# One step of a hybrid mLSTM/HGRN2 encoder on one core: HGRN score copies to ScalarE, a power on GpSimd for the head norms, later splits of fourth sums and embeddings

## The chip, the cores and the metric

The kernel runs on one core of one Trainium2 chip. The metric is device time in microseconds (us) of one execution, the median over several runs. Engines are named as in the profile: PE is TensorE's matmul array, PEld its weight loader, DVE is VectorE, ACT is ScalarE, POOL is GpSimd, and SP is the sync engine, which here only issues transfers (DMAs). Each engine works through a queue of its own in a fixed order; an instruction that waits holds everything behind it on that engine. All arithmetic is 32-bit; the matmuls take 32-bit operands split into a high and a low part.

## The reference, cut to what matters

One layer of a streaming encoder is computed for a prompt (512 frames of a new stream) and a sample (32 frames of a running stream). Both go through the same `_trunk`; an mLSTM branch and an HGRN2 branch run side by side and are merged. The parts that the change touches are the HGRN2 branch, the merge gates and the embeddings:

```python
xn = _rmsnorm(h, norm_g[l])
proj = xn @ w_in[l]
u, v_m, z_m, ig_pre, fg_pre, q_h, f_h, i_h, g_h, ga, gb = jnp.split(proj, _split_points(), axis=-1)
...
lfh = jnp.log(lb + (1.0 - lb) * jax.nn.sigmoid(f_lin))
kh = (1.0 - lb) * jax.nn.sigmoid(-f_lin)
qh = jax.nn.silu(q_h.astype(f32))
oh, S_new = _hgrn(to_heads(qh), to_heads(kh), to_heads(i_h.astype(f32)), to_heads(lfh), S0[l].astype(f32))
oh = _head_rmsnorm(oh.transpose(0, 2, 1, 3), hnorm_g[l].astype(f32)) * jax.nn.silu(g_h.astype(f32))
yb = oh.astype(x.dtype) @ w_brh[l]
y = jax.nn.sigmoid(ga) * ya + jax.nn.sigmoid(gb) * yb
h = h + y @ w_out[l]
h = h + jax.nn.sigmoid(h @ w_pg[l]) * (p[l] @ w_ple[l])
```

```python
def _hgrn_chunk(S, inp):
    q, k, v, lf = inp
    ...
    g = jnp.cumsum(lf, axis=2)
    dec = jnp.exp(jnp.where(causal, g[:, :, :, None, :] - g[:, :, None, :, :], -jnp.inf))
    a = jnp.einsum('bhtc,bhtsc,bhsc->bhts', q, dec, k)
    o = jnp.einsum('bhtc,bhce->bhte', q * jnp.exp(g), S) + jnp.einsum('bhts,bhse->bhte', a, v)
```

There are 8 HGRN heads of 128 channels. Each head's output is normalised by the root of its mean square over 128 channels (`_head_rmsnorm`). The embeddings `p` have 256 channels and are multiplied with `w_ple` at the end.

## The kernel before, in words

**Stages.** After the input norm the kernel works through four mLSTM heads (up to about 630 us), then through the HGRN loop with the merge gates (to about 960 us), and then through the dense products `yb` (w_brh), `o` (w_out), `ple` (w_ple) and `pg` (w_pg), the last mLSTM memories and the final norm.

**Precision.** `split` (line 101) and `split_piece` (125) divide a 32-bit operand into a high part, which is a copy on ACT (lines 103 and 130), and a low part, the difference, which is a subtraction on DVE (lines 104 and 131). Each product is three matmuls: high by high, high by low, low by high.

**Input products in pairs.** Class `Two` (387) computes two output tiles of `xn @ w_in` by a scheme with seven block products in place of eight. Besides the plain quarters a11, a12 and a22 of the weights it needs four sums of quarters, s1 to s4, which are made first and then split like the others. A block is 12 matmuls on PE. In the HGRN loop the pairs are "early" (all but the first): `begin` (397) loads one quarter by SP (line 402) and adds the other by an accumulating transfer that POOL issues (403), for s1 and s3. s2 is one more addition on DVE (`form`, 454, helper line 448). The fourth sum, s4, is s2's tile with another quarter added by an accumulating transfer that POOL issues as soon as s2 has been split (460); it uses the same buffer. The sums have five buffers (NSUM). After each block `keep` (496) copies the result from PSUM to a tile `t` on ACT (499), or `put` (502) combines it with an earlier one (506, 508, 510).

**The order of the blocks.** Class `Pump` (551) puts the blocks of all pairs into one list by due times. A pair's blocks fall due at 0 (a11), 1 (a12), 4 (s2, with s1's split), 5 (s1), 6 (s3), 9 (a22) and 10 (s4), and the next pair starts at 7. In the steady state the order is s2, s1, s3 of one pair, a11, a12 of the next, a22, s4 of the first, then s2 of the next. `prepare` (580) makes the weights, that is, emits loads, sums and splits, for the blocks up to AHEAD = 3 past the one that is about to run. `steps` (596) calls it before each block. The ACT instructions of a preparation are put behind the last `km` copy of the HGRN chain (`pump.behind`, 498), by `issue_after`.

**The HGRN chain.** `chain(h)` (1483) is the code of one head; the values that it yields say how many half blocks of the pump run on PE in between. The decay products within a chunk of 128 frames are built over seven levels c = 1, 2, 4, ..., 64. At each level ACT copies a strided key part to `km` (1500), PE multiplies it with the queries into a PSUM tile `pl` (1511), DVE multiplies decays into keys and queries (1535) and copies the scores whose pair of frames belongs to this level from PSUM into `at`, under a mask (`copy_predicated`, 1542). `at` is cleared by POOL before (1487). At the fifth level the sample's 32 frames are added (1519 to 1546). The previous head is finished inside the chain at that level too: `finish(h - 1)` (1654) transposes the normalised output on PE (`hoT`, 1659 and 1660) and multiplies by the gate. After the last level POOL cuts `at` to its two strict triangles `aa` (`triangle`, 1476, line 1479). PE transposes keys and values (`ht`, 1587), forms the state (`su`, 1606) and the output (`ho`, 1630 to 1634). Then the head norm follows: sums of squares on ACT (1641, 1642), a scaling (1643), `rsqrt` on five columns (160; integer first guess at 164 and 165, three Newton rounds at 167 to 169) and two multiplications (1645 and 1651), all on DVE.

**Merge gates and embeddings.** The last eight pairs of the pump are `ga` and `gb`. `merge_a` (1445) takes the sigmoid on ACT (1446), loads a `ya` tile and multiplies on DVE (1449); the eight products are collected in `gated`. Lines 1685 to 1690 load two embedding tiles `p` and split them into `ps0` and `ps1`, under `issue_after` on the third last product. `ple_units` (1692) uses them.

**Who orders what.** Within `tc.manual_schedule` the engines named there keep the order of the program; in the HGRN loop that is PE alone. Everything else is ordered ahead of the run by a scheduler that goes by readiness and by place in the program; `tc.high_priority()` puts instructions ahead of that place. `tc.issue_after(x)` puts instructions behind x. Semaphores and waits for buffers follow from the data.

Of the kernel before, what the change touches and what calls it, by code (L numbers as in the profile page):

```python
# [9 lines left out]
F32 = mybir.dt.float32  # L10
# [4 lines left out]
ALU = mybir.AluOpType  # L15
AX = mybir.AxisListType

P = 128
# [3 lines left out]
NP = 512  # L22
# [6 lines left out]
NB = NP // P  # L29
VW = HD + 4  # L30
VH = VW // 2
EPS = 1e-6
# [12 lines left out]
LEAD = 3  # L45
NPIECE = 5
AHEAD = 3
SCRATCH = 1024
RAWAHEAD = 4
WQ = 256  # L50
# [14 lines left out]
def hybrid_step(ctx: ExitStack, tc: tile.TileContext, a, o):  # L65
    nc = tc.nc
    V, S, G, PE = nc.vector, nc.scalar, nc.gpsimd, nc.tensor

    cp = ctx.enter_context(tc.tile_pool(name="cp", bufs=1))
# [8 lines left out]
    def slot(name, dt=F32):  # L78
        return sp.tile([P, SLOT], dt, tag="s", name=name)
# [5 lines left out]
    def small(name, shape, dt=F32, bufs=2, tag=None):  # L85
        return tp.tile(shape, dt, tag=tag or name, name=name, bufs=bufs)
# [11 lines left out]
    def paux(name):  # L98
        return pa.tile([P, 2, 512], F32, tag="a", name=name)

    def split(src, name):
        hi, lo = slot(name + "h", F32R), slot(name + "l", F32R)
        S.copy(hi[:, :T], src)
        V.tensor_tensor(lo[:, :T], src, hi[:, :T].bitcast(F32), ALU.subtract)
        return hi, lo
# [54 lines left out]
    def rsqrt(y, v, p, n, iters=3):  # L160

        t = small("rsq_t", [P, 8], I32)
        u = small("rsq_u", [P, 8])
        V.tensor_scalar(t[:p, :n], v.bitcast(I32), 1, None, ALU.logical_shift_right)
        V.tensor_scalar(y.bitcast(I32), t[:p, :n], -1, 0x5F3759DF, ALU.mult, ALU.add)
        for _ in range(iters):
            V.tensor_tensor(u[:p, :n], y, y, ALU.mult)
            V.scalar_tensor_tensor(u[:p, :n], u[:p, :n], -0.5, v, ALU.mult, ALU.mult)  # L168
            V.scalar_tensor_tensor(y, u[:p, :n], 1.5, y, ALU.add, ALU.mult)
# [29 lines left out]
    G.memset(ones, 1.0)  # L199
    zero4 = cp.tile([P, 4], F32, name="zero4")  # L200
    G.memset(zero4, 0.0)
    one4 = cp.tile([P, 4], F32, name="one4")
    G.memset(one4, 0.0)
    G.memset(one4[:, 0:1], 1.0)
# [125 lines left out]
    class One:  # L330
# [56 lines left out]
    class Two:  # L387
# [45 lines left out]
        def make(self, *forms):  # L433
            def go(raw):
                with tc.high_priority() if self.apart else nullcontext():
                    for form in forms:
                        if form not in self.w:
                            self.form(form, raw)

            return go  # L440

        def form(self, form, raw):
# [108 lines left out]
    class Pump:  # L551
# [28 lines left out]
        def prepare(self, upto):  # L580
            while self.made < min(upto, self.limit or len(self.order)):
                b = self.order[self.made]
                while self.begins and self.begins[0][0] <= self.made:
                    self.begins.pop(0)[1].begin()
                if b[1]:
                    need = self.loads.index(b[1][-1]) + 1
                    for u, i in self.loads[self.loaded : need + RAWAHEAD]:
                        self.raw[u, i] = raw_piece(w_in[u][:, i * WP : (i + 1) * WP], f"wi{u}r{i}")
                    self.loaded = max(self.loaded, min(need + RAWAHEAD, len(self.loads)))
                if b[2]:  # L590
                    after = self.pairs if isinstance(self.todo[self.ids[self.made][0]], Two) and self.pairs else self.behind
# [596 lines left out]
    with tc.manual_schedule(engines={mybir.EngineType.Activation, mybir.EngineType.DVE, mybir.EngineType.PE}):  # L1188
# [15 lines left out]
        for k in range(KD):  # L1204
            t = xt[k]
# [129 lines left out]
    with tc.manual_schedule(engines={mybir.EngineType.PE}):  # L1335
        for h in range(MH):
# [44 lines left out]
    NA = NP // 2  # L1381
# [12 lines left out]
    gbs, yas, gated = [None] * KD, [None] * KD, []  # L1394
# [88 lines left out]
    def chain(h):  # L1483

        tf, kk, q0, qq, kq, ii = (hs[h][k] for k in ("tf", "kk", "q0", "qq", "kq", "ii"))
        at = tp.tile([P, NA + P], F32, tag="bc", name=f"at{h}")
        G.memset(at, 0.0)
        snap = small("snap", [P, 2, QUADS, NS], bufs=1, tag="ksm")
        dg = small("dg", [P, 5])
        told = tf[:, :T]  # L1490
# [3 lines left out]
        for li, c in enumerate(LEVELS):  # L1494
            smp = li == QUADS
            n = HB if smp else NA
# [12 lines left out]
            pn = paux(f"pl{h}{c}")  # L1509
# [16 lines left out]
            with tc.high_priority():  # L1526
                for t, lo, m, first, _ in sides:

                    x = view(
                        kk, lo + first * c, ((qoff + (1 - 2 * first) * c, 2), (2 * c, m), (1, c))  # L1530
                    )
                    d = bass.AP(
                        t.tensor, t.offset + 1 - first, [list(t.ap[0]), [2 * first - 1, 2], [2, m], [0, c]]
                    )
                    V.tensor_tensor(x, x, d, ALU.mult)  # L1535
                if told.shape[-1] == 2 * (nb + na):
                    t = told.rearrange("p (n t) -> p n t", t=2)
# [4 lines left out]
                V.copy_predicated(at[:, :n], lmask[:, li, :n], pn[:, 0, :n])  # L1542
# [8 lines left out]
            if li == 0:  # L1551

                yield 1
                pn = paux(f"pd{h}")
# [22 lines left out]
        ov = kq  # L1577
        osb = small("osb", [P, P])
# [25 lines left out]
        for b in range(NB):  # L1604
            c = slice(b * P, (b + 1) * P)
# [22 lines left out]
        for b, (c, i, j) in enumerate(chunks):  # L1628
            d = slice(b * P, (b + 1) * P)
# [13 lines left out]
        V.tensor_scalar(hv, hv, 1.0 / P, EPS, ALU.mult, ALU.add)  # L1643
        rsqrt(hr, hv, P, 5)
        V.tensor_tensor(
            ov[:, :NP].rearrange("p (b e) -> p b e", b=NB),
            ov[:, :NP].rearrange("p (b e) -> p b e", b=NB),
            hr[:, :NB].rearrange("p (b o) -> p b o", o=1).to_broadcast([P, NB, P]),
            ALU.mult,
        )  # L1650
        V.tensor_scalar(osb, osb, hr[:, NB : NB + 1], None, ALU.mult)
        hs[h].update(ov=ov, osb=osb)

    def finish(h):
# [31 lines left out]
    for k in range(2):  # L1686
        t = slot(f"p{k}")
        with tc.issue_after(gated[-3].ins):
            nc.sync.dma_start(t[:, :T], a["pT"][k])
            ps_.append(split(t[:, :T], f"ps{k}"))  # L1690

    def ple_units(n):
# [24 lines left out]
    for f in range(KD):  # L1717
        t = slot(f"h1{f}")
# [167 lines left out]
```

## Time and profile before

| what | us |
|---|---|
| median of 3 runs | 1140.07 (1138.1 to 1141.18) |
| the profiled execution's own time | 1136.01 |
| its span, from the first to the last instruction | 1134.3 |
| PE busy in the span | 1116.8 |
| DVE busy | 896.5 |
| ACT busy | 680.2 |
| POOL busy | 185.9 |

The granted TensorE clock was 1.0 of full speed in nearly the whole span. The profile is one execution; times in it run from the start of its span. An engine that is idle shows in brackets how long it was idle before an instruction and what ended that: `[2.48 <-DMA p<-in_pT]` is 2.48 us of idle time ended by the transfer of `p`. A group's row has the line, the engine, the operation, `out<-in` by the program's names, the count, the busy time and the mean duration in ns. A row of waits has the waiting engine and line, whom it waited for, the total in us, how many times, and the longest.

### The profile page before, as it was taken

Reading aid. Unit: us, or ns where it says so; the run is one execution under the profiler, and the core shown is the slowest. Engines: PE = TensorE matmul, PEld = TensorE weight load, DVE = VectorE, ACT = ScalarE, POOL = GpSimd, SP = SyncE. Lnnn points to the kernel's source line nnn. Section 1 sums busy time; section 2 is a strip of 40 time slices with the busy share of each in tenths; the row PEclk is TensorE's granted clock in tenths of the full one; section 3 lists DMA queues with packets and bytes.
Section 4 is the critical chain, followed back from the end, with each engine's and each line's share of the span. In section 5 each row is a group of like instructions: output and inputs, shape, how many; then the busy total and the mean of one; then the engine's idle time right before and its main releaser. Section 6 shows DMA issues by size and latency. Waiting matters only on the chain.

```text
span 1134.3 us, 24068 instructions
## 1 busy us (share of the span) xinstructions
PE 1116.8 (98%) x8849; PEld 1101.4 (97%) x8849; DVE 896.5 (79%) x2027; ACT 680.2 (60%) x1537; POOL 185.9 (16%) x363
## 2 busy tenths in 40 slices
PE   9999999999999999999999999999999999999998
PEld 8999999999999999999999999999998999999998
DVE  6887998576896786976888699999999867654585
ACT  5677557655666555665665477677766657333462
POOL 4842010100010100101000122223232220000000
PEclk9999999999999999999999999999999999999999
DMA  7134224323344142552767766666666686332743
GB/s 236 56 96 133 79 75 159 118 95 106 132 152 151 49 131 105 158 168 69 239 163 234 180 145 143 138 140 140 148 149 165 174 222 172 113 103 70 269 141 116
DMA packets 91006, 159.68 MB, mean 141 GB/s; under 512 B 10245, under 2 KB 17797, under 8 KB 90889
## 3 DMA queue, kind: packets, MB, share of 16 engines
q1 hardware_dynamic: 80928, 140.27, 38.3%
q0 software_dynamic: 9792, 17.83, 10.1%
q8 instruction: 69, 1.13, 0.4%
q14 instruction: 49, 0.39, 0.1%
q10 hardware_dynamic: 168, 0.06, 0.0%
HBM read 133.21 MB, written 24.91 MB: 139 GB/s over the span
## 4 chain that ended last, share of the span: by engine, by line
PE 78%; DVE 10%; DMA 5%; ACT 3%; issue 2%; POOL 0%; SPq 0%; ACTq 0%; DVEq 0%
PE d L485 29%; PE ya L151 8%; PE pg L1736 4%; PE q L151 4%; PE yb L151 4%; PE o L151 4%; PE C L902 4%; PE k L151 4%; DMA ws<-in_w_in 3%; PE sc L862 3%; PE nm L1077 2%; PE pl L1511 2%; PE d L370 1%; DVE cv L634 1%; PE ple L151 1%
## 5 line engine op out<-in xcount | busy, mean ns | idle before, releaser
L403 POOL DMA_DIRECT2D ws<-in_w_in x46 | 40.3, 876 | 230.3 <-DVE rsq_u L168 30.3
L499 ACT COPY t<-d 128x272 f32<-128x272 f32 x126 | 47.7, 379 | 3.2 <-PE d L485 3.1
L1535 DVE TENSOR_TENSOR hkq<-hkq,q 128x288 f32<-128x288 f32 (+1 forms) x96 | 40.8, 432 | 3.9 <-PE pl L1519 1.0
L634 DVE SCALAR_TENSOR_TENSOR cv<-ub,vec,cv 128x547 f32<-128x547 f32 x48 | 40.4, 842 | 1.3 <-ACT cv L629 0.6
L1511 PE MATMUL pl<-hkq,km 128*128 128x128 f32 x224 | 38.0, 292 | 1.8 <-ACT km L1500 1.7
L1511 PEld LDWEIGHTS pl<-hkq,km 128*128 128x128 f32 x224 | 31.1, 189 | 3.9 <-ACT km L1500 3.4
L1500 ACT COPY km<-hkq 128x256 f32<-128x256 f32 x56 | 24.0, 428 | 15.6 <-DVE hkq L1535 6.2
L1006 DVE SCALAR_TENSOR_TENSOR c<-c,wi,Cs 128x258 f32<-128x258 f32 x32 | 15.3, 479 | 20.0 <-PE Cs L1004 19.8
L460 POOL DMA_DIRECT2D ws<-in_w_in x22 | 23.2, 1055 | 41.0 <-DVE ws272l L131 27.4
L914 ACT COPY Co<-C 128x258 f32<-128x258 f32 x32 | 10.4, 378 | 29.1 <-PE C L902 22.3
L1145 DVE TENSOR_TENSOR y<-ya,y 128x272 f32<-128x272 f32 x48 | 19.1, 436 | 10.3 <-PE ya L151 9.2
L1542 DVE COPY_PREDICATED at<-lmask,pl 128x256 f32<-128x256 uint8 (+1 forms) x56 | 25.3, 451 | 0.0
L1088 ACT COPY y<-nm 128x516 f32<-128x516 f32 x16 | 9.5, 591 | 21.6 <-PE nm L1077 21.5
L799 POOL COPY vsm<-vt 128x96 f32<-128x96 f32 x16 | 6.0, 382 | 88.2 <-ACT vt L510 44.7
L1479 POOL TENSOR_SCALAR_AFFINE_SELECT aa<-at 128x128 f32<-128x128 f32 x32 | 18.8, 621 | 8.9 <-DVE at L1542 8.9
L1077 PE MATMUL nm<-vhl,sh 128*128 128x258 f32 x112 | 18.3, 285 | 0.0
L1036 DVE BATCH_NORM_STATS2 bs<-y 128x6 f32<-128x512 f32 (+1 forms) x20 | 13.8, 688 | 5.5 <-ACT y L1088 5.5
L1723 DVE TENSOR_TENSOR h<-o,h 128x272 f32<-128x272 f32 x16 | 6.3, 436 | 14.5 <-PE o L151 14.5
L978 POOL CAST vhl<-one 128x4 fp32r<-128x4 f32 x8 | 2.0, 244 | 95.8 <-PE nm L1077 95.8
L876 ACT CAST sh<-dm 128x512 fp32r<-128x512 f32 (+3 forms) x16 | 7.3, 459 | 16.6 <-DVE dm L870 16.6
L1641 ACT ACTIVATE osq<-kq 128x128 f32<-128x128 f32 x32 | 9.8, 305 | 12.3 <-DVE kq L1636 12.1
L1710 DVE TENSOR_TENSOR gb<-yb,gb 128x272 f32<-128x272 f32 x16 | 6.3, 436 | 13.1 <-PE yb L151 13.1
(4490 smaller groups left out, 5072.9 us busy)
## 6 DMA issues: line engine op xcount, KB each, us to landing
ws<-in_w_in POOLq DMA_DIRECT2D x68, 256.0 KB, 4.8
ws<-in_w_in SPq DMA_DIRECT2D x46, 256.0 KB, 3.6
ya_d<-y SPq DMA_DIRECT2D x32, 272.0 KB, 2.7
y<-ya_d SPq DMA_DIRECT2D x24, 272.0 KB, 3.7
c<-in_C SPq DMA_DIRECT2D x16, 258.0 KB, 3.9
out_Cp<-Co SPq DMA_DIRECT2D x16, 258.0 KB, 2.5
out_Cs<-c SPq DMA_DIRECT2D x16, 258.0 KB, 2.8
x<-in_xT SPq DMA_DIRECT2D x8, 272.5 KB, 4.7
```

Of the source, the lines that this page charges most:

```text
L151: PE.matmul(both[b][:m, :TH], part(w, off + k * step, m, x), xx[:, half(b)], start=(k == 0 and j == 0), stop=(k == n - 1 and j == 2),)
L403: G.dma_start(t, w_in[u][:, i * WP : (i + 1) * WP], accum_op=ALU.add)
L485: PE.matmul(ps, ww[:, c], xx, start=(start and k == 0 and j == 0), stop=end, skip_group_check=not start,)
L499: S.copy(t, ps)
L634: V.scalar_tensor_tensor(cv[:, :547], ub[:, j : j + 547], vcol(V_CW + 4 * ft + j), cv[:, :547], ALU.mult, ALU.add)
L862: PE.matmul(pn[:, 0, :n], ks[f][x][:, j * P : (j + 1) * P], qs[f][y][:, NS + j * P : T], start=(f == 0 and i == 0), stop=(f == KH - 1 and ...
L902: PE.matmul(pn[g][:, :VH], kw[b][x][:, f * P : (f + 1) * P], vv[b][y][:, g * VH : (g + 1) * VH], start=(b == 0 and j == 0), stop=(b == NB ...
L1077: PE.matmul(pn[:, g, :VH], st[j][x][:, (i - j) * P : (i - j + 1) * P], vv[j][y][:, g * VH : (g + 1) * VH], start=(j == 0 and q == 0), stop ...
L1511: PE.matmul(pn[:, 0, b * P : (b + 1) * P], km[:, b * P : (b + 1) * P], view(qq, b * P, ((2 * c, P // (2 * c)), (HB + c, 2), (1, c))), star ...
L1535: V.tensor_tensor(x, x, d, ALU.mult)
L1542: V.copy_predicated(at[:, :n], lmask[:, li, :n], pn[:, 0, :n])
L1736: PE.matmul(ps, part(w, k * P, P, x), xx[:, c], start=(k == 0 and j == 0), stop=(k == KD - 1 and j == 2))
```

## The change

Four edits are made in one step.

1. *Scores.* At the first level and at the last one the masked copy on DVE is replaced by copies on ACT: one of 128x256 at the first level, and two of 64 partitions by 2x64 columns at the last. At the first level more is copied than before; the later triangles and levels take it away or write over it. Since the first level now writes the first 256 columns of `at`, POOL clears only the other 128.
2. *Norm.* The scaling moves from DVE to POOL, and the first guess with its three Newton rounds becomes a power of -0.5 on POOL with one Newton round on DVE (`newton` has the default `iters=1`; the 5 is the number of columns). The whole, with the multiplications, gets high priority. A constant of 128x5 is set at the start.
3. *Fourth sums.* The preparation of an early pair's s4 is held back while it is more than one block earlier than LATE = 2 allows: it is made two blocks ahead and no longer three. What follows it in the list waits for it, and is prepared in the same step.
4. *Embeddings.* The split of both tiles stands under `issue_after` on the last product `gated[-1]` instead of the third last; the loads stay where they were.

```diff
+LATE = 2
...
-    def rsqrt(y, v, p, n, iters=3):
...
+        newton(y, v, p, n, iters)
+
+    def newton(y, v, p, n, iters=1):
+
+        u = small("rsq_u", [P, 8])
         for _ in range(iters):
             V.tensor_tensor(u[:p, :n], y, y, ALU.mult)
             V.scalar_tensor_tensor(u[:p, :n], u[:p, :n], -0.5, v, ALU.mult, ALU.mult)
             V.scalar_tensor_tensor(y, u[:p, :n], 1.5, y, ALU.add, ALU.mult)
...
+    mhalf = cp.tile([P, 5], F32, name="mhalf")
+    G.memset(mhalf, -0.5)
...
+            go.late = self.early and not self.alone and forms == ("s4",)
             return go
...
             while self.made < min(upto, self.limit or len(self.order)):
                 b = self.order[self.made]
+                if getattr(b[2], "late", False) and self.made > upto - LATE:
+                    break
...
-        G.memset(at, 0.0)
+        G.memset(at[:, NA:], 0.0)
...
-                V.copy_predicated(at[:, :n], lmask[:, li, :n], pn[:, 0, :n])
+                if li == 0:
+                    S.copy(at[:, :NA], pn[:, 0, :NA])
+                elif c == P // 2:
+                    for d, e in ((slice(0, c), slice(c, P)), (slice(c, P), slice(0, c))):
+                        S.copy(
+                            at[d, :NA].rearrange("p (b t) -> p b t", b=2)[:, :, e],
+                            pn[d, 0, :NA].rearrange("p (b t) -> p b t", b=2)[:, :, e],
+                        )
+                else:
+                    V.copy_predicated(at[:, :n], lmask[:, li, :n], pn[:, 0, :n])
...
-        V.tensor_scalar(hv, hv, 1.0 / P, EPS, ALU.mult, ALU.add)
-        rsqrt(hr, hv, P, 5)
-        V.tensor_tensor(
...
+        with tc.high_priority():
+            G.tensor_scalar(hv, hv, 1.0 / P, EPS, ALU.mult, ALU.add)
+            G.tensor_tensor(hr, hv, mhalf, ALU.pow)
+            newton(hr, hv, P, 5)
+            V.tensor_tensor(
...
+            V.tensor_scalar(osb, osb, hr[:, NB : NB + 1], None, ALU.mult)
...
         with tc.issue_after(gated[-3].ins):
             nc.sync.dma_start(t[:, :T], a["pT"][k])
+        with tc.issue_after(gated[-1].ins):
             ps_.append(split(t[:, :T], f"ps{k}"))
```

More of the change, by code (lines that the diff above doesn't have):

```diff
@@ L162, in rsqrt @@
         t = small("rsq_t", [P, 8], I32)
-        u = small("rsq_u", [P, 8])
         V.tensor_scalar(t[:p, :n], v.bitcast(I32), 1, None, ALU.logical_shift_right)
         V.tensor_scalar(y.bitcast(I32), t[:p, :n], -1, 0x5F3759DF, ALU.mult, ALU.add)
+        newton(y, v, p, n, iters)
+    def newton(y, v, p, n, iters=1):
+        u = small("rsq_u", [P, 8])
         for _ in range(iters):
@@ L1642, in chain @@
         S.activation(osq, osb, AF.Square, accum_out=hv[:, NB : NB + 1])
-        V.tensor_scalar(hv, hv, 1.0 / P, EPS, ALU.mult, ALU.add)
-        rsqrt(hr, hv, P, 5)
-        V.tensor_tensor(
[L1646 to L1651, printed above, removed]
+        with tc.high_priority():
[3 more added lines that the diff above has]
+            V.tensor_tensor(
+                ov[:, :NP].rearrange("p (b e) -> p b e", b=NB),
+                ov[:, :NP].rearrange("p (b e) -> p b e", b=NB),
+                hr[:, :NB].rearrange("p (b o) -> p b o", o=1).to_broadcast([P, NB, P]),
+                ALU.mult,
+            )
+            V.tensor_scalar(osb, osb, hr[:, NB : NB + 1], None, ALU.mult)
         hs[h].update(ov=ov, osb=osb)
```

## The prediction

> **What bounds the kernel now.** I read the page first: its first part says which engine is full. Columns: busy time, share of the span, instructions.
>
> ```profile
> PE 1116.8 (98%) x8849; PEld 1101.4 (97%) x8849; DVE 896.5 (79%) x2027; ACT 680.2 (60%) x1537; POOL 185.9 (16%) x363
> ```
>
> TensorE (PE) is the bound, with 1134.3 - 1116.8 = 17.5 us idle in all. Work taken from VectorE (DVE), ScalarE (ACT) or GpSimd (POOL) is therefore worth only the TensorE idle time that it ends. Next the windows, busy time of each engine per stretch, for how much of that idle time lies in the HGRN loop:
>
> ```profile
> 630.00:840.00 210.00, 209.19 (x1684) 206.87 (x1683) 195.50 (x532) 147.16 (x402) 58.29 (x83) 1.00 0.65 147
> 840.00:930.00 90.00, 85.91 (x687) 84.50 (x686) 73.30 (x185) 57.22 (x144) 23.57 (x32) 1.00 0.70 175
> 630.00:960.00 330.00, 325.11 (x2605) 321.05 (x2603) 290.92 (x754) 224.17 (x586) 83.60 (x117) 1.00 0.66 156
> 960.00:1110.00 150.00, 150.00 (x1193) 149.75 (x1193) 90.97 (x180) 66.55 (x131) 0.00 (x0) 1.00 0.44 141
> ```
>
> After the stretch's length come PE, its weight loader (PEld), DVE, ACT and POOL. In the loop (630 to 960 us) PE is idle for 330 - 325.11 = 4.9 us and the loader for 330 - 321.05 = 9.0 us. Most of that lies in 840 to 930 us, the last head and its followers. DVE is 93% busy up to 840 us, yet PE misses only 0.8 us there: a crowded DVE costs almost nothing. After 960 us PE is full. So 9.0 us is the most that all edits can bring together. The third view, the waits from 640 to 960 us, names that time (total, times, longest, us), PE's own first; these three are all that it has:
>
> ```profile
> PE pl L1511 <- ACT km L1500: 1.7, 4, 0.7
> PE d L485 <- ACT t L499: 1.6, 1, 1.6
> PE hoT L1660 <- DVE osb L1651: 1.4, 1, 1.4
> ```
>
> and the loader's, where the last kind stands six times, 1.2 us in all:
>
> ```profile
> PEld pl L1511 <- ACT km L1500: 3.4, 7, 0.9
> PEld d L485 <- ACT t L499: 2.1, 2, 1.8
> PEld hoT L1660 <- DVE osb L1651: 1.7, 1, 1.7
> PEld d L485 <- DVE wa1253l L131: 0.2, 1, 0.2
> ...
> PEld d L485 <- DVE wa1252l L131: 0.2, 1, 0.2
> ```
>
> Matmul ends are modelled, so I take the true loss of each to lie between its PE and its PEld line.
>
> **Fourth sums (s4) later.** The longest case: ACT splits the result of an accumulating transfer,
>
> ```profile
> 868.21 0.62 ACT L130 CAST ws480h<-ws 128x512 fp32r<-128x512 f32 x1 [2.80 <-DMA ws<-in_w_in]
> ```
>
> and PE waits for the copy `km` that stands behind that cast on ACT, while the split itself is used later:
>
> ```profile
> 869.19 0.39 PE L1511 MATMUL pl<-hkq,km 128*128 128x128 f32 x1 [0.73 <-ACT km L1500]
> ...
> 874.56 0.29 PE L485 MATMUL d<-xh,ws480h 128*128 128x272 f32 x1
> ```
>
> So 2.80 us of ACT and 0.73 us of PE go to a split that is needed 874.56 - 868.83 = 5.7 us after its cast. Prepared one block later, s4 stands behind the copies of one more block. A block is 12 matmuls, and the loop runs 2605 in 330 us, so 1.5 us; where chain work lies between, more. That ends about half of such a wait or all of it, and the 5.7 us still cover the delay. No DMA moves: the accumulation is issued with s2, and the pair's first loads belong to the next block, which was never ahead of s4. Behind the later s4 stands the next pair's s2, in the same step as before. Together with the DVE time that the norms free, this is worth the pl line, 1.7 to 3.4 us; I take the middle, 2.5.
>
> **Norms.** Per head DVE does twelve small steps now: one scaling, two integer steps, three Newton rounds of three; then two multiplications. One head's chain on DVE, first and last step:
>
> ```profile
> 709.92 0.16 DVE L1643 TENSOR_SCALAR hv<-hv 128x5 f32<-128x5 f32 x1
> ...
> 719.75 0.28 DVE L1651 TENSOR_SCALAR osb<-osb,hr 128x128 f32<-128x128 f32 x1
> ```
>
> POOL's work at that time, two transfer issues and the idle time before them:
>
> ```profile
> 710.44 0.86 POOL L403 DMA_DIRECT2D ws<-in_w_in  x1 [3.87 <-DVE hv L1643]
> 718.47 0.89 POOL L403 DMA_DIRECT2D ws<-in_w_in  x1 [7.17 <-DVE at L1542]
> ```
>
> and the last transpose that reads the norm's result, in this head and in head 6:
>
> ```profile
> 721.32 0.27 PE L1660 MATMUL hoT<-anti,osb 128*128 128x128 f32 x1
> ...
> 878.99 0.33 PE L1660 MATMUL hoT<-anti,osb 128*128 128x128 f32 x1 [1.44 <-DVE osb L1651]
> ```
>
> The chain takes 10.1 us (709.92 to 720.03), because other DVE work is put between its 0.16 us steps; its reader follows 1.3 us later without a wait, and only in head 6 with one. `newton` is called with 5 columns and its default of one round, so nine steps go: 9 x 0.16 = 1.4 us a head. Two GpSimd steps come. A power stands in no row of this trace. The bounds are 0 and the longest clear, and I take 0.3 us a step, from the nearest shape:
>
> ```profile
> L852 POOL TENSOR_TENSOR qt<-qf,wi x16: 251/254/391, 95.3 to 526.3; 128x32 f32<-128x32 f32 x16
> L1487 POOL MEMSET at<- x8: 423/1112/1147, 350.9 to 830.2; 128x384 f32 x8
> ```
>
> (Shortest, median, longest, ns.) The steps should go in behind the first L403 issue, at 711.3, and give the root at about 712; three Newton steps (0.5), the two multiplications (0.7 and 0.3) and one product between them then end by 714. Added waits: POOL waits for ACT's last square, with transfer issues queued behind it; DVE waits for POOL, with weight splits and level products behind it. Of that wait up to 1.9 us (712 less the old scaling's end at 710.1) can be idle on DVE, which has 1.4 us a head less to do. The hoT wait goes: 1.4 to 1.7 us, I take 1.6; PE's order shows nothing that is late next there. The small waits, for splits that DVE's crowd delays, go by a quarter: 0.3 of 1.2 us.
>
> **Copies to ScalarE, smaller clear.** DVE loses two predicated copies a head, whose time is worth nothing directly, as said. ACT gains one 128x256 read of PSUM and two of 64x128; the nearest row:
>
> ```profile
> L499 ACT COPY t<-d 128x272 f32<-128x272 f32 x59 | 22.4, 380 | 2.5 <-PE d L485 2.4
> ```
>
> At most 3 x 0.38 = 1.1 us a head, on an engine that works 224 of 330 us. The last level's pair falls into ACT's fullest place, before this copy and its reader:
>
> ```profile
> 730.65 0.58 ACT L1590 COPY hkq<-ht 128x512 f32<-128x512 f32 x1
> ```
>
> ```profile
> 732.02 0.89 PE su L1606 x8
> ```
>
> The copy ends at 731.23, so 0.76 us more fits into the 0.79 us left, and below nothing there is no gain, since PE doesn't wait there. I cost it at nothing; without that cover it is at most 0.5 us x 8. A third of POOL's clear and one small constant cost nothing beside its idle time.
>
> **Embeddings split later.** The load on SP's queue, and the ACT half of the split:
>
> ```profile
> 912.91 0.42 SPq L1689 DMA_DIRECT2D p<-in_pT  x1
> ```
>
> ```profile
> 917.24 0.65 ACT L103 CAST ps0h<-p 128x544 fp32r<-128x544 f32 x1 [2.48 <-DMA p<-in_pT]
> ```
>
> The DVE half, between the sixth (gated[-3]) and the last product:
>
> ```profile
> 931.03 0.73 DVE L1449 TENSOR_TENSOR ya<-ya,ga 128x544 f32<-128x544 f32 x1
> 931.67 0.72 DVE L104 TENSOR_TENSOR ps0l<-p,ps0h 128x544 fp32r<-128x544 f32 x1
> ...
> 952.15 0.73 DVE L1449 TENSOR_TENSOR ya<-ya,ga 128x544 f32<-128x544 f32 x1
> ```
>
> and its first use:
>
> ```profile
> 954.85 0.29 PE L151 MATMUL ple<-ps0l,wple00h 128*128 128x272 f32 x1
> ```
>
> The cast waits 2.48 us for its transfer and holds ACT, and some 4 us later PE waits for a copy `t` from the same queue:
>
> ```profile
> 921.30 0.39 PE L485 MATMUL d<-xfh,ws384h 128*128 128x272 f32 x1 [1.62 <-ACT t L499]
> ```
>
> But see what the ordering block binds: the product at 931.03 is DVE's; the DVE half comes right behind it, the ACT half 14 us ahead. So only the DVE half is bound and only it moves, behind the product at 952.15. **I cost the ACT stall as staying**, 0 of 1.6. The two DVE halves end at about 953.5 and 954.2, before 954.85; the splits of PLE weights that they push back by up to 1.4 us can make PE late by 0 to 1.4. I take 0.3, since other matmuls can be put ahead.
>
> **The sum** is -2.5 - 1.6 - 0.3 + 0.3 = **-4.1 us**. On the profiled execution, 1136.01 us (span 1134.3 and 1.7 around it), that gives 1131.9. The median of the runs is 1140.07, 4.06 above that execution; I carry the difference over: **1136.0 us**. By PE's lines alone the sum is -1.7 - 1.4 + 0.3 = -2.8, by the loader's -3.4 - 1.7 - 1.2 + 0.3 = -6.0. The Trainium skill, Perfetto Trace Analysis, section Identifying the Most-Contended Engine, calls matmul busy time a bad measure of headroom and LDWEIGHTS busy time a good one; by that rule the -6.0 would stand, 1134.1 us.
>
> **Rivals.**
> 1. *The move to GpSimd doesn't help.* POOL's clear of one shape takes 423 to 1147 ns, and the two new steps lie on the chain. If the norm ends where it does now, the hoT gain and the small waits are lost: -2.5 + 0.3 = -2.2, 1137.9 us. Against it: six Newton steps and what lies between them are gone. The Trainium skill, Perfetto Trace Analysis, section Optimizing Scalar/DVE Operations, says that GpSimd and VectorE share an SBUF read port, so that moving work between them might not help; by that rule this rival is the result, and the trace shows only POOL's varying times.
> 2. *The ACT half moves too, or its transfer lands in time.* Then the `t` wait goes as well: -4.1 - 1.7 = -5.8, 1134.3 us. For it: the s4 cast before it holds ACT no longer. Against: its load is issued at 912.91, whatever ACT does.
> 3. *Slower: the norm stands behind the wrong transfer.* If POOL's order has the two steps behind the second L403 issue, they start at 719.4; with 0.6 for them, 0.5 for Newton, 0.7 and 0.3 for the multiplications and some 0.3 between engines, osb is ready at 721.8 and more wherever DVE is taken, say 722.4, for a reader at 721.32: 1.1 us late, in seven heads 7.7. With the pl gain and the split: +7.7 - 2.5 + 0.3 = +5.5, 1145.6 us. It decides from a root later than about 719. For it: POOL spends most of a head waiting for these issues. Against: priority, and an input that was there by 709.92, 8.5 us before that issue.
>
> **Chances.** 0.3% of 1140 us, 3.4 us, is about what a measurement can tell from no change. Forecast 0.40 (three quarters of it beyond 3.4 us), rival 1 0.20, rival 2 0.20, rival 3 0.15, another order of ACT and DVE, either way, 0.05. Faster 0.30 + 0.20 + 0.02 = 0.52; same 0.10 + 0.20 = 0.30; slower 0.15 + 0.03 = 0.18. The range goes from all 9.0 us gone, 1131.0, to rival 1 with 0.5 us x 8 of late ACT copies on it, 1142.0; rival 3 is left out.
>
> **What would show it.** Right: no ACT wait over 1.5 us for an s4 transfer; hoT without a wait, and osb some 5 us earlier in each head; the ps0h cast still waiting near 917 us, with the `t` wait behind it; ps0l right behind the last product. Wrong: DVE waiting microseconds for GpSimd's root, km or hoT waits in several heads, PE idle near 954 us, or a changed order before 630 us.

## The result, and the profile after

The changed kernel takes **1156.38 us** (median of four runs, 1155.73 to 1156.51) against 1140.61 us before (four runs, 1138.1 to 1141.18): ratio 1.014, 95% interval 1.0122 to 1.0158. It is slower by 1.4%, and the prediction (1136.0, range 1131 to 1142) was wrong in sign. The profiled execution took 1156.41 us (span 1154.7) against 1136.01 before, so the traces differ by 20.4 us, 4.6 us more than the medians.

The first part of the page, and the windows of the loop:

```profile
PE 1123.9 (97%) x8849; PEld 1105.1 (96%) x8849; DVE 888.1 (77%) x1939; ACT 687.2 (60%) x1561; POOL 192.2 (17%) x380
```

```profile
630.00:840.00 210.00, 198.64 (x1562) 193.91 (x1562) 176.26 (x438) 142.32 (x390) 58.19 (x89) 0.99 0.60 134
840.00:930.00 90.00, 86.25 (x688) 84.48 (x687) 71.83 (x170) 57.33 (x158) 26.57 (x37) 1.00 0.68 165
630.00:960.00 330.00, 310.90 (x2441) 304.19 (x2441) 266.00 (x638) 216.14 (x581) 90.87 (x133) 0.99 0.63 146
960.00:1110.00 150.00, 149.88 (x1192) 149.53 (x1191) 89.06 (x162) 68.86 (x134) 0.00 (x0) 1.00 0.47 150
```

Of the 20.4 us, 13.3 are idle time of TensorE (30.8 us in the span, 17.5 before). The other 7.1 are busy time for the same 8849 matmuls (1123.9 against 1116.8); the mean granted clock was 0.997 instead of 1.000, which by my estimate is 3.5 us of them. DVE does 8.4 us less work (896.5 to 888.1), as intended. In the loop TensorE is now idle for 330 - 310.90 = 19.1 us where it was 4.9, most of it from 630 to 840 us (11.4 us where it was 0.8): the heads in which a crowded DVE had cost nothing before. The tail after 960 us is as full as it was. TensorE's own waits from 660 to 960 us (total, times, longest, us):

```profile
PE pl L1521 <- ACT km L1510: 10.9, 14, 3.2
PE d L493 <- ACT t L507: 4.0, 1, 4.0
PE pl L1521 <- DVE q L1548: 2.3, 6, 0.4
PE ht L1607 <- POOL snap L1592: 1.6, 1, 1.6
```

The hoT wait is gone, as forecast. The km wait, which should have gone, grew from 1.7 to 10.9 us; the t wait from 1.6 to 4.0; two waits are new. Each head shows the same picture. GpSimd first, then DVE, ScalarE and TensorE of one head:

```profile
714.35 0.86 POOL L410 DMA_DIRECT2D ws<-in_w_in  x1 [2.16 <-DVE hg L514]
716.70 0.20 POOL L1663 TENSOR_SCALAR hv<-hv 128x5 f32<-128x5 f32 x1 [1.49 <-ACT osq L1661]
716.98 1.21 POOL L1664 TENSOR_TENSOR hr<-hv,mhalf 128x5 f32<-128x5 f32 x1
```

```profile
718.23 0.17 DVE L172 TENSOR_TENSOR rsq_u<-hr 128x5 f32<-128x5 f32 x1 [1.18 <-POOL hr L1664]
...
718.82 0.69 DVE L132 TENSOR_TENSOR wa2251l<-wi59r,wa2251h 128x512 fp32r<-128x512 f32 x1
719.42 0.68 DVE L1666 TENSOR_TENSOR kq<-kq,hr 128x512 f32<-128x512 f32 x1
720.03 0.79 DVE L1545 TENSOR_TENSOR hkq<-hkq,q 128x288 f32<-128x288 f32 x2
```

```profile
720.92 0.40 ACT L1510 COPY km<-hkq 128x256 f32<-128x256 f32 x1 [3.52 <-DVE hkq L1545]
```

```profile
721.38 0.39 PE L1521 MATMUL pl<-hkq,km 128*128 128x128 f32 x1 [0.84 <-ACT km L1510]
```

The steps stand behind the first L410 issue, where the prediction had them, and not behind the second (its third rival). But GpSimd waits 1.49 us more for ScalarE's last square, the power takes 1.21 us, DVE waits 1.18 us for it, and the second level's products, the copy `km` and TensorE's `pl` stand behind the Newton steps, a weight split and the large multiplication. The first head is the worst: there the issue ahead of the two steps waits for a transfer until 681.42, though ScalarE's last square ended at 679.6, and TensorE's longest km wait (3.2 us) follows.

```profile
681.42 0.87 POOL L410 DMA_DIRECT2D ws<-in_w_in  x1 [6.16 <-DMA ws<-in_w_in]
...
683.89 0.17 DVE L172 TENSOR_TENSOR rsq_u<-hr 128x5 f32<-128x5 f32 x1 [3.73 <-POOL hr L1664]
```

### The profile page after: what moved, and what is told of

Same layout as the page of the kernel before. It is cut to its first block, busy times and chain, and to the rows that moved or that the text cites. A ratio compares the mean times of both kernels' runs of the same rounds, so it can differ in the third digit from the quotient of the medians.

```text
span 1154.7 us, 24028 instructions
## 1 busy us (share of the span) xinstructions
PE 1123.9 (97%) x8849; PEld 1105.1 (96%) x8849; DVE 888.1 (77%) x1939; ACT 687.2 (60%) x1561; POOL 192.2 (17%) x380
## 4 chain that ended last, share of the span: by engine, by line
PE 73%; DVE 13%; ACT 4%; DMA 4%; issue 3%; POOL 2%; SPq 0%; ACTq 0%; DVEq 0%; POOLq 0%
PE d L493 25%; PE ya L152 8%; PE pg L1758 4%; PE q L152 4%; PE yb L152 4%; PE o L152 4%; PE C L912 4%; PE k L152 3%; PE sc L872 3%; DMA ws<-in_w_in 2%; PE nm L1087 2%; PE pl L1521 2%; DVE hkq L1545 2%; PE d L377 1%; DVE cv L644 1%
## 5 line engine op out<-in xcount | busy, mean ns | idle before, releaser
L410 POOL DMA_DIRECT2D ws<-in_w_in x46 | 41.0, 891 | 220.8 <-DMA ws<-in_w_in 42.6
L1521 PE MATMUL pl<-hkq,km 128*128 128x128 f32 x224 | 39.4, 298 | 13.5 <-ACT km L1510 10.9
L1521 PEld LDWEIGHTS pl<-hkq,km 128*128 128x128 f32 x224 | 30.9, 189 | 19.5 <-ACT km L1510 19.5
L1561 DVE COPY_PREDICATED at<-lmask,pl 128x256 f32<-128x256 uint8 (+1 forms) x40 | 18.0, 449 | 0.0
L1660 ACT ACTIVATE osq<-kq 128x128 f32<-128x128 f32 x32 | 9.9, 308 | 13.5 <-DVE kq L1655 13.3
L822 ACT ACTIVATE kf<-k 128x272 f32<-128x272 f32 x32 | 10.9, 392 | 9.4 <-PE k L152 9.4
```

What stands on the lines that cost most here:

```text
L410: G.dma_start(t, w_in[u][:, i * WP : (i + 1) * WP], accum_op=ALU.add)
L1521: PE.matmul(pn[:, 0, b * P : (b + 1) * P], km[:, b * P : (b + 1) * P], view(qq, b * P, ((2 * c, P // (2 * c)), (HB + c, 2), (1, c))), star ...
```

## The experiments

**First round: is it the norms?** From the picture above I held the norm block for nearly the whole loss, with the copies on ScalarE as rival. The four kernels, as edits:

```
e1_after_oldnorm  (changed kernel, norms of before)
-            G.tensor_scalar(hv, ...); G.tensor_tensor(hr, hv, mhalf, ALU.pow); newton(hr, hv, P, 5)
+        V.tensor_scalar(hv, ...); rsqrt(hr, hv, P, 5)
e2_before_norm    (kernel before, with the change's norm block alone)
e3_after_mult     (changed kernel; leaves the root out)
-            G.tensor_tensor(hr, hv, mhalf, ALU.pow)
+            G.tensor_tensor(hr, hv, mhalf, ALU.mult)
e4_norm_behind_level2  (changed kernel; Newton and both multiplications as scale(h))
+            if li == 1 and h:
+                with tc.issue_after(prod.ins):   # the level's last product
+                    scale(h - 1)
```

> The changed kernel with the norms as before: scaling, integer start and three Newton rounds on DVE, no priority; copies, later s4 and later embeddings stay. Theory: most of the loss is the norm block, whose Newton steps wait on DVE for the power on GpSimd ahead of the second level's product (2.1 us a head in seven heads, some 15, and some 2 more in the first head); left are the 2.3 us that the embeddings' copy t waits longer, a TensorE clock that falls after it, and the 1.6 us ht wait of the first head: 1141 to 1145 us, at most 0.4% over the kernel before. Rival: the copies on ScalarE delay km and the last level's pl (0.4 to 0.5 us a head of the 2.1 stand at waits that don't name GpSimd): 1146 to 1150.

> The kernel before with the new norm alone (scaling and power on GpSimd, one Newton round, multiplications, all with priority). Theory: it holds nearly all of the loss: 1152 to 1157 us. Rival, that the copies on ScalarE share it: 1147 to 1150. Were the norm innocent: 1138 to 1141.

> The changed kernel with a multiplication in the place of the power on GpSimd, so that the root is not computed; the order of the instructions is the same on every engine. Theory: DVE's wait for the power's 1.21 us is what PE sees, about 1.0 us a head in seven heads, and 1 to 2 us in the first: 1146 to 1149 us. Rival: the block itself (three Newton steps, a weight split and the multiplication of 0.7 us) ahead of the second level's product costs the time, with or without a wait for GpSimd: 1153 to 1156.

> The changed kernel with the power left on GpSimd, but Newton's round and the multiplications on DVE put behind the products of the next head's second level. Theory: the place of the wait is the cause, and nothing waits for the root there: the 15 us of the seven heads go, and the 3.2 us of the first head: 1139 to 1143 us. Rival: GpSimd's power costs time wherever it is read (the chain to osb, or the transfer issues queued behind it): above 1148.

Measured, against 1139.67 us before: e1 1156.15 (1.014, 1.0106 to 1.0174); e2 1146.49 (1.0048, 1.0031 to 1.0066); e3 1149.79 (1.0087, 1.0052 to 1.0121); e4 1158.7 (1.0168, 1.0122 to 1.0213). **The theory fell.** Without the norm block the loss is all there, and the block by itself makes less than half of it. What it said of the power itself held: with a multiplication of 0.20 us in its place, which leaves the root out, the time falls by 6.6 us, DVE's waits for it from 14.3 to 7.1 us (eight each):

```profile
L1664 POOL TENSOR_TENSOR hr<-hv,mhalf x8: 1197/1207/1210, 682.6 to 914.6; 128x5 f32<-128x5 f32 x8
...
  DVE rsq_u L172: 14.3, 8
```

(Power in the changed kernel: shortest, median, longest, ns; below, who waited for it.) In e1 and e4 TensorE's waits have other names in six heads: in e1 `d <- DVE ws274l` to `ws279l`, 1.2 to 1.3 us each; in e4 `d <- DVE wa1151l` to `wa1155l`, 1.5 us each. These are weight splits on DVE, late at places that the edits hardly touch. The priority on the block can't be the cause: without it the program has the same instructions in the same order on every engine.

**Second round: the other edits, each alone.**

```
e5_before_copies  before, with the copies on ScalarE and the smaller clear
e6_before_late    before, with LATE = 2, go.late and the break in prepare
e7_before_emb     before, with issue_after(gated[-1].ins) around the split
e8_after_nocopies changed kernel, with copy_predicated and the whole clear
```

> The kernel before with the copies on ScalarE and the smaller clear alone. The first four runs felled the theory that the norm block holds nearly all of the loss: without it the change still took 1156.15 us, with it alone 1146.49. New theory: what costs time is DVE's order, which every edit shifts: a DVE instruction that waits for another engine stands ahead of a weight split or a product that PE needs, so the prices of the edits do not add up, and this one alone costs little, 1138 to 1143 us. Rival: the copies on ScalarE cost a fixed time in every head, which is what the change without the norm shows: 1150 to 1156.

> The kernel before with the fourth sums prepared one block later alone. Theory of DVE's order: little, 1136 to 1141 us, as the splits ws27x stay ahead of the fifth level's product in DVE's order. Rival: the later s4 is what costs the 15 us of the change without the norm: 1150 to 1156.

> The kernel before with the embeddings split later alone. Theory: only the DVE half moves, and the ScalarE half goes on waiting for its transfer ahead of the copy t: 1138 to 1142 us. Rival: the later split moves the second load and the PLE matmuls and costs time by itself, with a TensorE clock that falls behind the wait: 1143 to 1146.

> The changed kernel without the copies on ScalarE and with the whole clear: norm, later s4 and embeddings stay. The norm alone gave 1146.49 us, all four 1156.38. If the copies bring the other 10 us (last level's pl late by 0.3 to 0.4 us a head, km behind the copies): 1145 to 1149 us. If the later s4 or the embeddings bring them: 1152 to 1157.

Against 1139.5 us before: copies alone 1140.61 (1.0011, 0.9994 to 1.0028); **later s4 alone 1154.27 (1.0125, 1.0094 to 1.0155)**; embeddings alone 1141.64 (1.0004, 0.9988 to 1.0021); the change without the copies 1152.45 (1.0103, 1.0065 to 1.0141). Copies and embeddings cost nothing by themselves. The edit that I had as the largest gain costs 14.8 us by itself: the rival won. TensorE's waits in e6, and DVE in one head:

```profile
PE d L487 <- ACT t L501: 2.8, 1, 2.8
PE d L487 <- DVE wa1154l L132: 1.9, 1, 1.9
PE d L487 <- DVE wa1153l L132: 1.9, 1, 1.9
PE d L487 <- DVE wa1151l L132: 1.8, 1, 1.8
PE d L487 <- DVE wa1180l L132: 1.8, 1, 1.8
PE d L487 <- DVE wa1152l L132: 1.8, 1, 1.8
PE d L487 <- DVE wa1155l L132: 1.8, 1, 1.8
PE pl L1515 <- ACT km L1504: 0.7, 4, 0.2
```

```profile
728.56 0.43 DVE L1539 TENSOR_TENSOR hkq<-hkq,q 128x256 f32<-128x256 f32 x1 [0.22 <-ACT t L501]
728.90 0.50 DVE L510 SCALAR_TENSOR_TENSOR hi<-d,t 128x16 f32<-128x16 f32 x2
729.32 0.42 DVE L1539 TENSOR_TENSOR hkq<-hkq,q 128x256 f32<-128x256 f32 x1
729.65 0.29 DVE L1542 TENSOR_TENSOR q<-q 128x136 f32<-128x136 f32 x1
729.86 0.43 DVE L1546 COPY_PREDICATED at<-lmask,pl 128x256 f32<-128x256 uint8 x1
730.20 0.22 DVE L1542 TENSOR_TENSOR q<-q 128x68 f32<-128x68 f32 x1
730.33 0.69 DVE L132 TENSOR_TENSOR wa1152l<-wi52r,wa1152h 128x512 fp32r<-128x512 f32 x1
```

The km wait did shrink, from 1.7 to 0.7 us, which is the gain that I forecast. But the split wa1152l, which TensorE wants at 729.2, stands behind both products of the last level, `hi`, a copy and parts of `q`. In the kernel before it stood ahead of them:

```profile
726.60 0.69 DVE L131 TENSOR_TENSOR wa1152l<-wi52r,wa1152h 128x512 fp32r<-128x512 f32 x1
727.77 0.43 DVE L1535 TENSOR_TENSOR hkq<-hkq,q 128x256 f32<-128x256 f32 x1 [0.49 <-ACT t L499]
```

Six such waits are 11.0 us. To them comes a clock that falls behind four of them, below.

**Third round: places or room, and the norm's place without the later s4.** e9 gives the late splits priority on DVE and leaves the orders of TensorE and SyncE as in e6. On GpSimd, unlike what its expectation says, two accumulating transfers change places in six heads (in e6 L462 is issued at 703.89 and L404 at 704.60; in e9, where each stands one line lower, L405 at 705.73 and L463 at 706.29), and six copies `t` move on ScalarE. e10 and e11 take the later s4 out; e12 also moves the ScalarE half of the embeddings' split.

```
e9_late_wa11first  (e6)
+            with tc.high_priority() if name.startswith(("wa115", "wa1180")) else nullcontext():
                 low = eng.tensor_tensor(lo[:, c], raw[:, c], hi[:, c].bitcast(F32), ALU.subtract)
e10_after_nolate   (changed kernel)
-            go.late = self.early and not self.alone and forms == ("s4",)
e11_norm2_nolate   (e4)   the same line out
e12_all            (e11)
+        with tc.issue_after(acts[-3].ins):      # the sixth sigmoid
+            S.copy(hi[:, :T], t[:, :T])
+        with tc.issue_after(gated[-3].ins):
+            V.tensor_tensor(lo[:, :T], t[:, :T], hi[:, :T].bitcast(F32), ALU.subtract)
```

> The kernel before with the later s4, and the DVE half of the first split of each next pair (wa1150l to wa1155l, wa1180l) given priority; TensorE's and GpSimd's orders are those of the later s4 alone. There wa1151l to wa1155l and wa1180l came 1.8 to 1.9 us after TensorE wanted them, 11.1 us in six waits, with a granted clock of 0.94 in the windows behind. Theory: the later s4 sets these splits back in DVE's line, behind the products of the last two levels, and nothing else of it costs time: 1137 to 1143 us. Rival: DVE has no room, so the wait moves to what the split is put ahead of (the products, km, pl): 1146 to 1152.

> The changed kernel with the fourth sums prepared where they were; norms, copies and embeddings as changed. Theory: the later s4 brings most of the loss and the norm's wait for the power the rest (alone 1154.27 and 1146.49 us, copies and embeddings alone nothing): 1145 to 1149 us. Rival: the norm and the copies meet on DVE and cost more together, as the 1152.45 us without the copies and the 1156.38 us with them suggest: 1150 to 1154.

> As the run without the later s4, and DVE's part of the norms put behind the products of the next head's second level, the power still on GpSimd. Theory: both causes are gone and what is left is near the kernel before: 1137 to 1142 us. Rival: the place of the norm isn't what costs time, or its place there costs as much (with the later s4 this place gave 1158.7): above 1145.

> As the run before it, with the ScalarE half of the embeddings' split bound behind the gate's sixth sigmoid on ScalarE and the DVE half back behind the sixth product. Theory: the wait for the transfer leaves ScalarE's line, so the copy t is no longer late, and TensorE wins 1.6 to 2.9 us and a fallen clock behind it: 2 to 4 us below the run before it, 1134 to 1139. Rival: the cast is late for the PLE matmuls or in the way of other copies: no gain or a loss.

Against 1140.49 us before: e9 1154.43 (1.0115, 1.009 to 1.0139); e10 1148.98 (1.0072, 1.0052 to 1.0092); e11 1140.24 (0.9995, 0.9983 to 1.0007); e12 1141.73 (1.0009, 0.9995 to 1.0023). e10 and e11 came as expected: the change without the later s4 loses 8.5 us, and DVE's part of the norms behind the second level's products wins 8.7 us back, with the power still on GpSimd. e4 had the same place and lost by the later s4. e12 missed: the cast no longer waits for p, but the next accumulating transfer (ws484) was then waited for, 7.8 us, and the `t` wait was 4.3 us. e9 missed too; the splits were in time, but TensorE waited somewhere else:

```profile
PE ht L1592 <- DVE at L1547: 13.2, 6, 2.5
PE d L488 <- ACT t L502: 3.5, 1, 3.5
```

```profile
765.92 0.43 DVE L1547 COPY_PREDICATED at<-lmask,pl 128x256 f32<-128x256 uint8 x1
766.25 0.30 DVE L1543 TENSOR_TENSOR q<-q 128x136 f32<-128x136 f32 x1
766.46 0.25 DVE L1669 SCALAR_TENSOR_TENSOR ob<-hoT,vec,hg 128x32 f32<-128x32 f32 x1
```

```profile
766.50 1.08 PE L1592 MATMUL ht<-ident,hi 128*128 128x128 f32 x4 [2.50 <-DVE at L1547]
```

When planning e13 I took the second half of `ob`, the last reader of `hoT`, for what `ht` waits for. The rows say otherwise: `ht` starts 0.15 us after the end of the copy `at` (766.35), which the view names, and 0.21 us before `ob` ends (766.71); the other five heads show the same. `ob` comes into it a step earlier. The tiles of `hoT`, `pl` and `ht` take turns in two PSUM buffers. In e6 `ob` stood ahead of the last level (727.75, the products at 728.56 and 729.32); in e9 these 0.25 us of work have slipped behind it, and in the program of e9 the first `ht` of these six heads has the buffer of the last level's `pl`, so that it must wait for the copy of these scores. In the first and the last head it has another buffer and doesn't wait. So either DVE lacks room, or two places are wrong.

**Fourth round: both places.**

```
e13_late_two_first  (e9);  e14_all_first  (e4, with e9's lines);  e15_before_first  (before, with e9's lines)
+        with tc.high_priority():
             V.scalar_tensor_tensor(ob[:, NS:T], ...)
             V.scalar_tensor_tensor(ob[:, :NS], ...)
```

> The kernel before with the later s4, the splits wa1150l to wa1155l and wa1180l given priority, and both halves of ob too. With the first priority alone the wait of 1.8 us went, but ht then waited 2.2 us for the second half of ob (0.25 us of DVE work, which frees ht's PSUM buffer) that stood behind the last level's copy. Theory: both waits come from places in DVE's order, not from work that DVE has no room for: with both put right, 1137 to 1143 us. Rival: DVE lacks the room, so a third place is late by as much: 1148 to 1155.

> The whole change (later s4, copies, power on GpSimd, later embeddings) with three places in DVE's order put right: DVE's part of the norms behind the second level's products, and the priorities of the run above. Theory: then nothing of the 16 us is left but the 2 to 4 us at the embeddings' copy t: 1137 to 1144 us. Rival: the later s4 costs time with the other edits in any order: above 1148.

> Control: the kernel before with the two priorities and nothing else, so that the run with the later s4 and these priorities can be read against it. Theory: nothing is late there now, so nothing is won or lost: 1137 to 1142 us. If the priorities win time by themselves, below 1136.

Against 1140.13 us before: **e13 1133.71 (0.9939, 0.9925 to 0.9953)**; e14 1146.8 (1.0051, 1.0037 to 1.0065); e15 1137.6 (0.9979, 0.9967 to 0.9991). The later s4 with two places put right is 20.6 us below the later s4 alone. It is faster than the kernel before, and than the control with the same priorities by 3.9 us. The control itself wins 2.5 us, where nothing was expected to be won; why is open. In e13 `ht` has the buffer of the level before and no longer waits. TensorE's waits that are left from 640 to 990 us:

```profile
PE d L488 <- ACT t L502: 3.1, 1, 3.1
PE pl L1516 <- ACT km L1505: 1.2, 2, 0.7
```

From 690 to 840 us, e6 first, then e13:

```profile
690.00:840.00 150.00, 139.90 (x1089) 137.69 (x1088) 136.13 (x372) 99.22 (x274) 41.28 (x60) 0.97 0.59 130
```

```profile
690.00:840.00 150.00, 150.00 (x1225) 149.77 (x1224) 147.28 (x416) 107.96 (x307) 49.00 (x63) 1.00 0.64 146
```

In e13 TensorE isn't idle at all and DVE is 98% busy; in e6 DVE was 91% busy and TensorE waited for it. So DVE had the room: the order was wrong, not the amount. The priorities move some instructions on GpSimd, ScalarE and SyncE too, so the gain belongs to the new order as a whole; what is shown of the two places is that the waits at them are gone. e14 missed: the whole change with three places put right still loses 6.7 us, with waits at km (7.3 us in eight, 4.9 of it from 840 us on), at the copy `t` (3.7 us) and at `ht <- snap` (2.6 us in two). The two longest km waits come behind a cast that waits for the transfer of an s4, which is what the later s4 was to end:

```profile
854.71 0.62 ACT L131 CAST ws479h<-ws 128x512 fp32r<-128x512 f32 x1 [2.47 <-DMA ws<-in_w_in]
855.69 0.71 PE L1522 MATMUL pl<-hkq,km 128*128 128x128 f32 x4 [1.97 <-ACT km L1511]
...
890.03 0.62 ACT L131 CAST ws488h<-ws 128x512 fp32r<-128x512 f32 x1 [3.75 <-DMA ws<-in_w_in]
891.01 0.38 PE L1522 MATMUL pl<-hkq,km 128*128 128x128 f32 x1 [2.13 <-ACT km L1511]
```

**Last runs.** e16 is e13 with e12's edit of the cast; e17 is the changed kernel with e13's two priorities.

> The later s4 with both priorities, and the ScalarE half of the embeddings' first split bound behind the gate's sixth sigmoid; the orders of TensorE, GpSimd and the load queue stay. The later s4 with the priorities alone took 1133.71 us, and its one long wait left is the copy t behind that cast, 3.1 us, with a granted clock of 0.89 in the window behind it. Theory: the wait for p's transfer was in the way; it goes, and some 2 to 5 us with it: 1129 to 1132 us. Rival, from the earlier try without the later s4, where the wait moved to the transfer of ws484 (7.8 us): 1133 to 1136.

> The changed kernel with the two priorities (wa115xl and wa1180l, both halves of ob) and nothing else. Theory: its own waits stand at km behind GpSimd's root and not at these two places, so little is won: 1152 to 1157 us. If the later s4 costs its time in the changed kernel at these same places, about what the change without the later s4 took or less: 1145 to 1149.

e16: 1133.98 against 1139.93 us (0.9947, 0.9934 to 0.9961), the same as e13. The rival held: ScalarE waited 4.9 us for ws484's transfer instead, `ACT ws484h`, and TensorE's longest `t` wait fell only to 1.5 us. e17: 1152.26 against 1139.58 us (1.0112, 1.0077 to 1.0147), at the lower edge of what was expected. By the medians of two rounds that is 4.1 us less than the changed kernel's 1156.38, but the intervals overlap (1.0122 to 1.0158 there): at most about a quarter of its loss hangs on these two places.

## Why the prediction was wrong, step by step

**Fourth sums, forecast -2.5, alone +14.8.** This step failed, where it says "that ends about half of such a wait or all of it, and the 5.7 us still cover the delay" and "in the same step as before". Both halves are true of s4 and s2 themselves: none of their splits is late in e6, and the km waits shrink. But DVE's and ScalarE's orders are written when the program is built, and one split that moves shifts the places of others: wa1151l to wa1155l and wa1180l fall behind the last level's products. I asked what the moved step needs, and not what else changes places in a line that is 93% full; "another order of ACT and DVE" stood among the chances with 0.05 and no price. With two places put right the edit brings -3.9 us against its control, near the term (-2.5, ends -1.7 and -3.4). ScalarE's waits for transfers of s4 from 640 to 960 us fall from 16.2 us in eleven (e15) to 6.4 in four (e13), TensorE's km waits from 4.1 to 1.2 (e15's trace is of its slowest execution, 1141.29, so the sizes are rough): the mechanism was right, the cover wrong. In the changed kernel the later s4 costs 7.4 us (1156.38 against e10's 1148.98). There it shows as longer km waits, 19.5 against 13.0 us on the loader's side; which places cause these is open, since e17's two priorities mend 4.1 us at most.

**Norms, forecast -1.9 with the small waits, alone +6.8.** The hoT wait went, but it is gone in e5, e6 and e15 too, which leave the norms alone. Two things failed. The power takes 1.21 us, not 0.3, which e3 values at 6.6 us. And the wait on DVE, of which "up to 1.9 us" a head "can be idle on DVE, which has 1.4 us a head less to do", had the right size (14.3 us in eight heads, 1.8 each) and was taken for free. DVE has time over in the sum, but not at that place: the second level's products stand behind the wait. e11 shows it: with the steps behind these products DVE waits for the root in two heads only (3.0 us), and 8.7 us are won back. The rival "the move to GpSimd doesn't help" took the gain away and saw no loss; the third rival saw a loss (+5.5 in all), but behind a later transfer. The Trainium skill's rule on a shared SBUF port (Perfetto Trace Analysis, Optimizing Scalar/DVE Operations), which I weighed for that rival, is not what costs the time here: e3's multiplication makes the same kind of access on GpSimd and is 6.6 us faster, and e11 keeps power and scaling on GpSimd and takes as long as the kernel before.

**Copies at nothing.** Right alone (1140.61). In company they may cost something: the changed kernel is 3.9 us slower than e8 by the medians of two rounds, but the intervals overlap, so that isn't shown.

**Embeddings.** Right: only the DVE half moves, the cast goes on waiting, alone the edit makes no difference. The stall that I took as staying was longer in the trace of the changed kernel:

```profile
936.56 0.64 ACT L104 CAST ps0h<-p 128x544 fp32r<-128x544 f32 x1 [3.62 <-DMA p<-in_pT]
```

```profile
940.62 0.60 PE L493 MATMUL d<-xfh,ws384h 128*128 128x272 f32 x1 [3.98 <-ACT t L507]
```

That the edit made it longer isn't shown: in e5 and e15, which leave the embeddings where they were, this `t` wait is 2.7 and 3.5 us. The 1.6 us of the kernel before come from an execution that was 4 us faster than the median.

**The sum.** Each edit was priced with the other edits' orders held still. Alone, the four give +6.8, +1.1, +14.8 and +2.1 us against the medians of their own rounds, 24.8 together (the 1.1 and the 2.1 lie within noise), and the change as a whole gives 15.8. They don't add: each one writes a new order. Within the change, the later s4 is worth 7.4 us and the place of the norms behind it 8.7 (e10, e11), 16.1 together, which is the whole loss. The Trainium skill's rule that LDWEIGHTS busy time, with MFU, is the measure of headroom (the same page, Identifying the Most-Contended Engine) would have made the forecast 1134.1, farther from the result: neither row says which waits a new order makes.

## What to carry to other kernels

Where engines' orders are written ahead and one of them is nearly full, an edit moves more than its own instructions: list what will change places on the full engine, and ask of each which reader it has and when. When an edit that should be harmless costs time in every head, look for the split or the 0.25 us step that slipped behind something, and give that one priority before giving up the edit; it turned the later s4 alone into a gain, and was not enough for the whole change. A wait for another engine goes where nothing urgent stands behind it; the sum of the busy time doesn't tell where that is.

## What the runs showed of the hardware

A power on GpSimd over 128x5 took 1197 to 1210 ns, a multiplication of the same shape in its place 195 to 201 ns: the operation costs, not the call.

The granted TensorE clock fell behind gaps in the middle of a busy loop. Two-microsecond windows of e6 around its 1.82 us wait, the clock in the third column from the right:

```profile
728.00:730.00 2.00, 1.26 (x11) 1.03 (x10) 1.78 (x7) 1.95 (x7) 0.55 (x2) 1.00 0.47 47
730.00:732.00 2.00, 0.92 (x4) 0.92 (x5) 2.00 (x7) 1.25 (x5) 1.62 (x3) 0.76 0.48 88
732.00:734.00 2.00, 2.00 (x11) 2.00 (x11) 2.00 (x6) 0.25 (x1) 1.00 (x2) 0.50 0.43 133
734.00:736.00 2.00, 2.00 (x16) 2.00 (x15) 0.91 (x2) 1.42 (x5) 0.00 (x0) 0.89 0.74 239
```

The clock lost here is at most 2 x (0.24 + 0.50 + 0.11) = 1.7 us, nearly as much as the wait. It didn't happen at every such wait: of the six 30 us windows of e6 that hold one, four have a mean of 0.94 to 0.96 (720 to 780 and 810 to 870 us) and two 1.00 (690 to 720, 780 to 810). In the changed kernel it happened behind its 3.2 and 4.0 us waits (0.51 from 688 to 690 us, 0.50 from 942 to 944). The Trainium skill (TensorE: Matmul & The Clock Gate, Part 1: The HAM clock gate) says that the clock halves after an idle window of about 3.4 us that runs freely, and warns of idle gaps above that. The halving agrees with the 0.50; the length doesn't, since 1.82 us was enough in some heads here, and 1.53 us in e4 (0.55 from 768 to 770 us), while nothing fell behind 2.47 us in e3 (1.00 from 686 to 692). Length alone doesn't decide it, and what else does is open. Where the clock falls, a wait of about 2 us costs nearly twice its length.
